# Hybrid encoder layer: value blocks multiplied in pairs of 512 columns, small tiles kept in the second weight slot

## The chip, the cores and the metric

One core of a Trainium2 chip runs the kernel in one launch. The metric is the device time of one execution in microseconds (us), the median of several executions. The core has a matrix engine (TensorE, PE), which reads on-chip memory (SBUF) and writes accumulation banks (PSUM); a vector engine (VectorE, DVE); a scalar engine (ScalarE, ACT); a general engine (GpSimd, POOL); and a sync engine (SyncE, SP) that issues most transfers.

## The reference

One layer of an encoder, sequence 2048, width 1024, all in float32:

```
mod = silu(c) @ w_ada + b_ada;  shift, scale, gate = split(mod, 3)
h   = rmsnorm(x, norm_w) * (1 + scale) + shift
proj = h @ w_in + b_in          # 4 attention parts, 5 mLSTM parts, 16 gate columns
attention: 8 heads of 64, on a 32 x 64 grid, 8 x 16 neighbourhood, bias table rpb, softmax
           times silu(z)
mLSTM:     4 heads of 128, q and k through a 5-tap convolution and silu, both directions,
           stabilised by log-gates; (fwd + bwd) * sigmoid(o), normalised per head, times silu(z)
out = rmsnorm(x + gate * (concat(attention, mLSTM) @ w_out), final_norm_w)
```

The mLSTM values and the output gates `o` of one head form one 256-column block of the projection (blocks 0 to 3), the attention's values two more (blocks 4 and 5), the mLSTM's k and q four (blocks 6 to 9, with the convolution).

## The kernel before, in words

**Numbers.** A float32 product is made of three matmuls. Each operand is split in a high part in the fast format fp32r and a low part, the rest; high x high, high x low and low x high are summed in PSUM (`mm3`, lines 638 to 640). With a depth of 1024 in eight slices that is 24 matmuls for one output tile. h lies in SBUF for the whole first phase, in four groups g of 512 tokens (`hhi`, `hlo`).

**Weights.** A block of weights is 1024 x 256. `raw_w` loads it in two halves of 512 KB into two raw buffers (line 203) and returns for each half a function that writes the high part (ACT, line 207) and the low part (DVE, line 208) into a weight slot. There are two slots, a and b; block n uses slot n % 2. Slot a has 272 columns, for the gate columns of block 0, and lives until the end; slot b is given up after the convolution.

**Start.** `start` stands in `manual_schedule`: there each engine's order is the order of the program text. It multiplies blocks 0 and 1 for all four token groups and block 2 for group 0. In its last group `next_w` loads and splits block 2 into slot a. Table fills (`table_fills`, line 758) and the store of each group's results (line 721, deferred to a later point by `defer` and `flush`) go out on SP as well.

**Value blocks.** `tok_blocks` does the rest of blocks 2 to 5, one block after the other, each by groups and each group by four tiles of 128 tokens: 24 matmuls with 256 moving columns, the tokens of h being the stationary operand, then one DVE addition of the bias out of PSUM (`vo_group` for blocks 2 and 3, line 710; `nav_group` for 4 and 5, line 673). The PSUM pool `pp` has four banks. The splits for the next block follow groups 1 and 2 of the present one. After each tile one step of `self.chain` is taken: first the gate computations (`gate_chain`, with exponential and logarithm at lines 827 and 828 and their user at line 830) mixed with the row of the output gate (`gate_row`: the vector c is loaded at line 587 and goes through Silu at line 588; lines 596 to 607), then the decay matrices (`decays`). Two stage tiles hold results until they are stored. Outside `manual_schedule` the framework's scheduler sets each engine's order, by priority and by its own estimates of when things are ready.

**Convolution and mixer.** `conv_blocks` multiplies blocks 6 to 9 with 512 moving columns. In `phase1b` the mLSTM runs per head in two passes (`ml_pass1`: states; `ml_pass2`: outputs, chunk by chunk), while `pump` lays matmuls of the remaining projections (line 1094, 512 moving columns) between its steps. Pass 1 loads a tile `kv` per chunk and multiplies its values by a weight, in place for one direction. Pass 2 fills a tile `hm` of four chunks (two buffers; lines 1366 to 1368), normalises it, transposes it on PE, and `end` (line 1407) multiplies the transposed group into the gate tile `zt` (two buffers), which is stored (line 1410) and then loaded anew (line 1326).

**Attention.** `phase2` stands in `manual_schedule` from `slot(0)` on. Per unit it makes scores on PE, adds a bias table and takes minima on DVE (line 1598), exponentials on ACT, sums, transposes on PE and values. The probabilities and their transposes go round a ring of ten tiles of 512 columns, four of them the buffers of `hm` and `zt`:

```python
for t in ring[4:] + ring[:4]:
    nc.gpsimd.memset(t, 0.0)
```

The bias tables of the first patch are loaded before `self.close()`, which ends the mixer.

Of the kernel before, what the change touches and what calls it, by code (L numbers as in the profile page):

```python
# [15 lines left out]
P = 128  # L16
# [3 lines left out]
NG = 4  # L20
# [38 lines left out]
class Kernel:  # L59
# [75 lines left out]
    def phase1(self):  # L135
        nc, tc = self.nc, self.tc
        left = ExitStack()
        right = ExitStack()
        ht012 = self.pool(left, "ht012", bufs=1)
        self.hpools = {g: ht012 for g in range(3)}  # L140
        self.hhi, self.hlo = [], []
        self.token_tiles(0)

        self.gcols = self.pool(right, "gcols", bufs=1, side="right")
        wa = self.pool(right, "wa", bufs=1, side="right")
        self.raw = self.pool(right, "raw", bufs=1, side="right")
# [3 lines left out]
        wb = self.pool(r1a, "wb", bufs=1, side="right")  # L150
        self.wslot = []
# [20 lines left out]
        self.tok_blocks(self.pool(toks, "chain", bufs=1, side="right"))  # L172
# [16 lines left out]
    def stage_tile(self, name):  # L189
        self.stages.reverse()  # L190
        return self.stages[1].tile([P, 1032], F32, tag="st", name=name).rearrange("p (o c) -> p o c", o=4)

    def load_w(self, blk, slot, halves=(0, 1)):
        for part in self.raw_w(blk, slot, halves):
            part()

    def raw_w(self, blk, slot, halves=(0, 1)):
        nc = self.nc
        hi, lo = self.wslot[slot]

        def part(half):
# [12 lines left out]
        return [part(half) for half in halves]  # L214

    def start(self, left):
# [316 lines left out]
        self.chain = iter(())  # L533
# [132 lines left out]
    def nav_group(self, blk, slot, g):  # L666
        nc = self.nc
        c0 = (blk - 4) * 256
        st = self.stage_tile(f"stv_{blk}_{g}")
        for o in range(4):  # L670
# [3 lines left out]
            next(self.chain, None)  # L674
            if o == 1:
                self.flush()
        dst = self.d_vna[g * GT : (g + 1) * GT, c0 : c0 + 256].rearrange("(o p) c -> p o c", p=P)
        self.defer(lambda: nc.sync.dma_start(dst, st[:, :, :256]))
# [17 lines left out]
    def vo_group(self, h, slot, g, first=None, brow=None, tops=(), stage=None):  # L696
# [5 lines left out]
        for o in range(4):  # L702
# [10 lines left out]
            next(self.chain, None)  # L713
            if o == 1:
                self.flush()
        nc.scalar.activation(st[:, :, 129:257], st[:, :, 129:257], AF.Sigmoid)
        dst = self.d_ck[h, 4 * g : 4 * g + 4, :, 128:385].rearrange("o p c -> p o c")
        if g == 0 and h < 3:
            (nc.scalar if h == 0 else nc.sync).dma_start(dst, st[:, :, 0:257])
        else:  # L720
            self.defer(lambda: nc.sync.dma_start(dst, st[:, :, 0:257]))

# [52 lines left out]
    def tok_blocks(self, chain_pool):  # L775
        self.wide = chain_pool.tile([P, 2 * D], F32, name="wide")
        self.chain = itertools.chain(self.gate_both(chain_pool), self.decays(chain_pool))
        order = [2, 3, 4, 5]
        next(self.chain)
        r = self.tables_begin(chain_pool)  # L780
        for n, blk in enumerate(order):
            parts = self.raw_w(blk + 1, (blk + 1) % 2)
            if blk < 5:
                self.load_bias(blk + 1)
            for g in range(1 if blk == 2 else 0, NG):
                if blk < 4:
                    self.vo_group(blk, blk % 2, g)
                else:
                    self.nav_group(blk, blk % 2, g)
                if g in (1, 2):  # L790
                    parts[g - 1](self.nc.vector)
                if blk == 2 and g == 3:
                    self.tables_bias(r)
# [4 lines left out]
    def gate_chain(self, pool, gates):  # L798
# [29 lines left out]
        nc.scalar.activation(a, a, AF.Ln, bias=1.0)  # L828
        lf = new("lf")
# [369 lines left out]

    def close(self):  # L1200
# [45 lines left out]
    def ml_pass1(self, ml, h):  # L1246
# [5 lines left out]
        def load(k):  # L1252
            t = tiles[k] = ml.tile([P, 257], F32, tag="kv", bufs=7, name=f"kv_{h}_{order[k]}")
            nc.sync.dma_start(t, self.d_ck[h, order[k], :, 0:257])

        def weight(k):
            c = order[k]
            v = tiles[k][:, 128:257]
            sides[k] = {d: v for d in range(2) if 0 <= c + 1 - 2 * d < NC}
            if len(sides[k]) == 2:  # L1260
                sides[k][1] = ml.tile([P, 129], F32, tag="wv", bufs=4, name=f"wv_{h}_{c}")
# [45 lines left out]
    def ml_pass2(self, ml, h):  # L1307
# [11 lines left out]
        def load_z(gi):  # L1319
# [4 lines left out]
            else:  # L1324
                t = self.mle.tile([P, 4, CH], F32, tag="zt", bufs=2, name=f"zt_{h}_{gi}")
# [135 lines left out]
    def phase2(self):  # L1461
# [91 lines left out]
        tabs = [p.tile([P, 960], F32, name=f"tab{i}") for i in range(4)]  # L1553
# [182 lines left out]
        for i in range(2):  # L1736
            load_q(i)
            for u in (2 * i, 2 * i + 1):
                load_tab(b0, u, nc.sync if i else nc.gpsimd)
        self.close()  # L1740
        pss = ExitStack()
# [3 lines left out]
        ring = [few.tile([P, 512], F32, tag=tag, bufs=bufs, name=f"ring_{i}") for i, (tag, bufs) in enumerate((("hm", 2), ("hm", 2), ("zt", 2), ("zt", 2)))]  # L1745
        ring += [p.tile([P, 512], F32, name=f"ring_{i}") for i in range(4, 10)]
        for t in ring[4:] + ring[:4]:
            nc.gpsimd.memset(t, 0.0)
# [118 lines left out]
        with self.tc.manual_schedule():  # L1867
            for m in range(len(patches) + 1):
# [96 lines left out]
```

## Time and profile before

| | |
|---|---|
| time, median of 3 runs | 1277.23 us (1277.06 to 1277.59) |
| the profiled execution's own time | 1276.39 us |
| its span, first to last instruction | 1274.5 us |
| PE busy | 1264.4 us, 99% |
| DVE / ACT / POOL busy | 790.3 / 537.7 / 201.7 us |
| granted TensorE clock, mean | 0.999 of full speed |

The stages on PE: start up to about 131 us, value blocks to 306, convolution to 491, mixer with projections to about 927, attention with the output projection to the end. An engine's busy time is the sum of its instructions' records; PE's records overlap one another, so the distance between starts says more than a record's length.

### The profile page before, as it was taken

To read this page: it belongs to the slowest core of one execution; us is meant where nothing else is said; L and a number is where in the kernel's file an instruction comes from. 1 tells how busy PE (TensorE), PEld (TensorE's weight loads), DVE (VectorE), ACT (ScalarE), POOL (GpSimd) and SP (SyncE) were. 2 spreads that over 40 slices of the span, in tenths; PEclk is the share of its full clock that TensorE was granted. 3 is DMA by queue.
4 is the path that set the end of the run, shared out by engine and by line. 5 is a ranking of instruction groups with operands and counts; after the bars stand their busy time and mean duration, and the time that the engine had idled before them with its cause. 6 is when DMAs were issued, how large, how long until landed. Compare 5 with 4: busy or idle time off the path is not lost.

```text
span 1274.5 us, 22948 instructions
## 1 busy us (share of the span) xinstructions
PE 1264.4 (99%) x8168; PEld 1095.4 (86%) x8168; DVE 790.3 (62%) x2391; ACT 537.7 (42%) x1182; POOL 201.7 (16%) x368
## 2 busy tenths in 40 slices
PE   9999999999999999999999999999999999999997
PEld 8999999999888888888888888888877888888886
DVE  7875542213667664267777778777556766767664
ACT  6642425442334222123323323324357565565552
POOL 0000003440000000000001001000424331332541
PEclk9999999999999999999999999999999999999999
DMA  9999947996678764745757867746677755655551
GB/s 366 335 309 286 283 147 198 249 245 180 180 180 189 165 154 115 207 131 164 204 160 207 251 189 215 240 149 186 207 249 266 230 162 160 203 177 176 176 173 67
DMA packets 217082, 259.08 MB, mean 203 GB/s; under 512 B 23435, under 2 KB 163595, under 8 KB 216968
## 3 DMA queue, kind: packets, MB, share of 16 engines
q1 hardware_dynamic: 149542, 190.09, 52.1%
q0 software_dynamic: 13616, 37.28, 8.9%
q10 hardware_dynamic: 53810, 30.24, 8.4%
q8 instruction: 65, 1.06, 0.3%
q14 instruction: 49, 0.40, 0.1%
HBM read 173.05 MB, written 92.72 MB: 209 GB/s over the span
## 4 chain that ended last, share of the span: by engine, by line
PE 95%; DVE 2%; ACT 1%; issue 1%; DMA 0%; DVEq 0%; ACTq 0%
PE pq L1094 27%; PE y L1676 14%; PE pc L639 5%; PE pc L640 5%; PE pc L638 5%; PE pO L1633 4%; PE pT L1618 3%; PE pvo L638 3%; PE pvo L640 3%; PE pvo L639 3%; PE pS L1587 3%; PE pvo L693 3%; PE pv L640 2%; PE pv L639 2%; PE pv L638 2%; PE pi L1346 2%
## 5 line engine op out<-in xcount | busy, mean ns | idle before, releaser
L1094 PE MATMUL pq<-hhi,whi_a 128*128 128x512 f32 x512 | 208.4, 407 | 0.0
L1094 PE MATMUL pq<-hlo,whi_a 128*128 128x512 f32 x512 | 207.8, 406 | 0.0
L1094 PE MATMUL pq<-hhi,wlo_a 128*128 128x512 f32 x512 | 207.2, 405 | 0.0
L1368 POOL TENSOR_TENSOR hm<-hm,ck 128x128 f32<-128x128 f32 x64 | 28.2, 440 | 580.3 <-DVE hm L1367 541.0
L1094 PEld LDWEIGHTS pq<-hhi,wlo_a 128*128 128x128 f32 x512 | 96.8, 189 | 16.7 <-issue 0.2
L1094 PEld LDWEIGHTS pq<-hlo,whi_a 128*128 128x128 f32 x512 | 96.7, 189 | 16.1 <-issue 0.4
L1094 PEld LDWEIGHTS pq<-hhi,whi_a 128*128 128x128 f32 x512 | 96.8, 189 | 15.9
L1599 ACT ACTIVATE ring<-ring,mn 128x480 f32<-128x480 f32 (+5 forms) x128 | 75.9, 594 | 55.8 <-DVE mn L1598 55.8
L1620 ACT ACTIVATE ring<-pT 96x384 f32<-96x384 f32 (+3 forms) x128 | 65.8, 514 | 63.5 <-PE pT L1618 62.0
L1676 PE MATMUL y<-hhi,wlo_a 128*128 128x512 f32 (+1 forms) x272 | 87.0, 394 | 0.2 <-ACT y L1683 0.2
L1676 PE MATMUL y<-hhi,whi_a 128*128 128x512 f32 x256 | 86.2, 408 | 0.0
L1349 ACT ACTIVATE num<-px,gtile 128x129 f32<-128x129 f32 x120 | 38.7, 367 | 105.2 <-PE px L1344 91.5
L1522 POOL DMA_DIRECT2D v<-d_vna x158 | 78.7, 505 | 15.6 <-issue 4.4
L1618 PEld LDWEIGHTS pT<-ident,ring 128*128 128x128 f32 (+2 forms) x416 | 51.1, 136 | 19.2 <-ACT ring L1620 3.7
L1618 PE MATMUL pT<-ident,ring 128*128 128x128 f32 (+2 forms) x416 | 66.2, 272 | 0.0
L638 PE MATMUL pvo<-whi_b,hhi 128*128 128x256 f32 x224 | 63.6, 284 | 0.0
L1598 DVE CUSTOM_DVE_ANT_0 ring<-pS,tab 128x480 f32<-128x480 f32 (+5 forms) x128 | 61.9, 539 | 2.6 <-PE pS L1587 2.4
L640 PE MATMUL pvo<-whi_b,hlo 128*128 128x256 f32 x224 | 63.1, 282 | 0.0
L639 PE MATMUL pvo<-wlo_b,hhi 128*128 128x256 f32 x224 | 63.0, 281 | 0.0
L934 ACT ACTIVATE dec<-dec,gtile 128x128 f32<-128x128 f32 x128 | 41.3, 391 | 46.9 <-POOL dec L927 43.2
L673 DVE TENSOR_TENSOR stv<-pv,brow 128x256 f32<-128x256 f32 x32 | 13.6, 425 | 71.8 <-PE pv L640 71.8
L710 DVE TENSOR_TENSOR stvo<-pvo,brow 128x256 f32<-128x256 f32 x60 | 24.7, 418 | 50.7 <-PE pvo L640 40.0
(343 smaller groups left out, 3331.3 us busy)
## 6 DMA issues: line engine op xcount, KB each, us to landing
ck<-d_ck SPq DMA_DIRECT2D x64, 384.5 KB, 3.6
rawq<-in_w_main_dram SPq DMA_DIRECT2D x28, 512.0 KB, 5.2
raw<-in_w_main_dram SPq DMA_DIRECT2D x18, 512.0 KB, 6.2
kv<-d_ck SPq DMA_DIRECT2D x64, 128.5 KB, 3.0
dec<-d_mneg SPq DMA_DIRECT2D x32, 256.0 KB, 6.0
d_ck<-dec ACTq DMA_DIRECT2D x32, 256.0 KB, 6.9
qs<-d_qna SPq DMA_DIRECT2D x30, 256.0 KB, 3.9
xr<-in_x_p_dram POOLq DMA_DIRECT2D x15, 512.0 KB, 3.9
```

Of the source, the lines that this page charges most:

```text
L638: nc.tensor.matmul(ps, lhi(k), rhi(k), start=(k == 0), stop=False)
L639: nc.tensor.matmul(ps, lhi(k), rlo(k), start=False, stop=False)
L640: self.mark = nc.tensor.matmul(ps, llo(k), rhi(k), start=False, stop=(k == KT - 1))
L934: nc.scalar.activation(t[:, o, :], t[:, o, :], AF.Exp, bias=self.cols["g"][:, d, h, c : c + 1])
L1094: self.mark = nc.tensor.matmul(patch_ps(ps) if patch else ps, w, self.htok(h, g, k, patch), start=(k == 0 and n == 0), stop=(k == KT - 1 a ...
L1522: queue.dma_start(chunks[key][r * nkc : (r + 1) * nkc, :], rows[r])
L1598: nc.vector.tensor_tensor_reduce(pt[:, :nk], ps, tabs[ct][:, j * nk : (j + 1) * nk], 1.0, 3e38, ALU.add, ALU.min, mn)
L1599: nc.scalar.activation(pt[:, :nk], pt[:, :nk], AF.Exp, bias=mn, scale=-1.0, accum_out=sums[:, j : j + 1])
L1618: nc.tensor.transpose(ps[:cs, i, :], U[u][j][:, i * cs : (i + 1) * cs], self.ident)
L1620: nc.scalar.activation(t[:cs, :nch, :], ps[:cs, :nch, :], AF.Copy)
L1633: nc.tensor.matmul(po[j * HD : (j + 1) * HD, ct, :], v[:n, h * HD : (h + 1) * HD], pt[j][:n, i, :], start=(i == 0), stop=(i == nch - 1))
L1676: nc.tensor.matmul(y, m[:, k, :], w[k][:, cs], start=(k == 4 and n == 0), stop=(k == 3 and n == 2))
```

## The change

Blocks 2 and 3, and blocks 4 and 5, are multiplied together where both are at hand: one matmul has 512 moving columns, 256 from each slot, and fills a whole PSUM bank (`pair_group`). The order of groups becomes (2,1) (3,0) [2+3: 2] [2+3: 3] (3,1) (4,0) [4+5: 1] [4+5: 2] [4+5: 3] (5,0). Each block's raw halves are loaded and split at other points (`splits`, `turns`; the raw halves of block 3 in `next_w`). Four stage tiles take the place of two in that stage. The two weight slots become the halves of one tile per part, which stays to the end. Once the convolution is done, slot 2 holds the `kv` tiles, the `zt` tiles and the four bias tables (`spare`); the values weighted in pass 1 all go to tiles of their own; `end` writes into `hm` and that is stored; the fourth table is loaded after `close()`. In `gate_chain` a step ends between the logarithm and its user. The ring keeps the two `hm` buffers and eight tiles of its own, and DVE clears the upper half of each, in the written order.

```diff
@@ phase1
-        for nm, pl in (("a", wa), ("b", wb)):
-            self.wslot.append(tuple(pl.tile([P, KT, 272 if nm == "a" else 256], F32R, name=f"w{part}_{nm}") for part in ("hi", "lo")))
+        self.wpair = tuple(wa.tile([P, 2, KT, 272], F32R, name=f"w{part}") for part in ("hi", "lo"))
+        self.wslot = [tuple(part[:, j] for part in self.wpair) for j in range(2)]
...
+        held, more = self.stages, self.pool(toks, "stage2", bufs=2, side="right")
+        self.stages = [*held, more, more]
@@ start, next_w
-            for part in self.raw_w(2, 0):
+            self.parts = []
+            for half, part in enumerate(self.raw_w(2, 0)):
                 yield
                 part(nc.vector)
+                self.parts.append(self.raw_part(3, 1, half))
@@ new
+    def pair_group(self, blk, g):
+        sts = [self.stage_tile(f"st2_{blk + j}_{g}") for j in range(2)]
+        hi, lo = self.wpair
...
+        for o in range(4):
+            ps = self.pp.tile([P, GT], F32, tag="pp", name=f"p2_{blk}_{g}_{o}")
+            self.mm3(
+                ps.rearrange("p (a c) -> p a c", a=2),
+                lambda k: self.hhi[g][:, k, o * P : (o + 1) * P],
+                lambda k: self.hlo[g][:, k, o * P : (o + 1) * P],
+                lambda k: hi[:, :, k, :256],
+                lambda k: lo[:, :, k, :256],
+            )
+            for j, st in enumerate(sts):
+                row, part = self.brows[(blk + j) % 2], ps[:, 256 * j : 256 * j + 256]
...
+                    self.evicted = nc.vector.tensor_add(st[:, o, :256], part, row)
+                next(self.chain, None)
+            next(self.mid, None)
+            if o == 1:
+                self.flush()
@@ tok_blocks
-        order = [2, 3, 4, 5]
+        order = [(2, 1), (3, 0), (2, 2), (2, 3), (3, 1), (4, 0), (4, 1), (4, 2), (4, 3), (5, 0)]
+        both = ((2, 2), (2, 3), (4, 1), (4, 2), (4, 3))
+        def splits(rest, after):
+            for _ in range(rest):
+                yield
+            for part in self.parts:
+                part(self.nc.vector)
+                yield
+            if after:
+                self.parts = self.raw_w(*after)
...
+        turns = {0: (1, (4, 0)), 4: (0, (5, 1)), 5: (0, (6, 0)), 9: (0, None)}
@@ gate_chain
         nc.scalar.activation(a, a, AF.Ln, bias=1.0)
+        yield
         lf = new("lf")
@@ new
+    def spare(self, half, start, n):
+        return self.wslot[1][half].rearrange("p a b -> p (a b)").bitcast(F32)[:, start : start + n]
@@ ml_pass1
-            t = tiles[k] = ml.tile([P, 257], F32, tag="kv", bufs=7, name=f"kv_{h}_{order[k]}")
+            t = tiles[k] = self.spare(0, k % 7 * 257, 257)
...
+            sides[k] = {d: ml.tile([P, 129], F32, tag="wv", bufs=8, name=f"wv_{h}_{c}_{d}") for d in range(2) if 0 <= c + 1 - 2 * d < NC}
@@ ml_pass2
-                t = self.mle.tile([P, 4, CH], F32, tag="zt", bufs=2, name=f"zt_{h}_{gi}")
+                t = self.spare(1, gi % 2 * 512, 512).rearrange("p (a q) -> p a q", q=P)
...
-            nc.vector.scalar_tensor_tensor(z, ps, self.mlw[:, h : h + 1], z, ALU.mult, ALU.mult)
-            src = zt[gi]
+            src = hm[gi]
+            nc.vector.scalar_tensor_tensor(src.rearrange("p a q -> p (a q)"), ps, self.mlw[:, h : h + 1], z, ALU.mult, ALU.mult)
@@ phase2
-        tabs = [p.tile([P, 960], F32, name=f"tab{i}") for i in range(4)]
+        tabs = [self.spare(half, start, 960) for half, start in ((0, 0), (0, 960), (1, 1024), (1, 0))]
...
         self.close()
+        load_tab(b0, 3)
...
-        for t in ring[4:] + ring[:4]:
-            nc.gpsimd.memset(t, 0.0)
+        ring += [p.tile([P, 512], F32, name=f"ring_{i}") for i in range(2, 10)]
...
         with self.tc.manual_schedule():
+            for t in ring:
+                nc.vector.memset(t[:, 256:], 0.0)
```

## Rows read from the trace of the kernel before

**Rows 1.** The page: PE's busy line, and the chain that ended last, by engine.

```profile
PE 1264.4 (99%) x8168; PEld 1095.4 (86%) x8168; DVE 790.3 (62%) x2391; ACT 537.7 (42%) x1182; POOL 201.7 (16%) x368
...
PE 95%; DVE 2%; ACT 1%; issue 1%; DMA 0%; DVEq 0%; ACTq 0%
```

**Rows 2.** The waits of PE, first of five rows: us in total, times, longest.

```profile
PE pvo L436 <- ACT hhi L404: 1.2, 2, 0.8
```

**Rows 3.** Tile pv (blocks 4, 5): ns min/median/max, first and last start.

```profile
L638 PE MATMUL pv<-whi_a,hhi x128: 276/280/283, 215.0 to 260.0; 128*128 128x256 f32 x128
...
L638 PE MATMUL pv<-whi_b,hhi x128: 279/281/285, 260.4 to 305.6; 128*128 128x256 f32 x128
```

**Rows 4.** The chain in order of time, convolution and projections: start, us, what.

```profile
306.09 0.23 PE pc L638
...
309.59 0.23 PE pc L638
...
491.53 41.70 PE pq L1094 x180
```

**Rows 5.** Tile pvo, PE, 119 to 215 us: block 2 in slot a.

```profile
L638 PE MATMUL pvo<-whi_a,hhi x96: 277/280/388, 130.6 to 166.3; 128*128 128x256 f32 x96
```

**Rows 6.** DVE in order of time, 115 to 200 us; in brackets the idle time before.

```profile
129.16 1.23 DVE L208 TENSOR_TENSOR wlo_a<-raw,whi_a 128x1024 fp32r<-128x1024 f32 x1 [3.60 <-ACT whi_a L207]
...
130.63 1.21 DVE L208 TENSOR_TENSOR wlo_a<-raw,whi_a 128x1024 fp32r<-128x1024 f32 x1
...
138.18 0.29 DVE L830 SCALAR_TENSOR_TENSOR wide<-wide 128x128 f32<-128x128 f32 x1 [1.08 <-ACT wide L828]
...
152.56 1.22 DVE L208 TENSOR_TENSOR wlo_b<-raw,whi_b 128x1024 fp32r<-128x1024 f32 x1 [5.31 <-ACT whi_b L207]
153.71 0.42 DVE L710 TENSOR_TENSOR stvo<-pvo,brow 128x256 f32<-128x256 f32 x1
```

**Rows 7.** SP's transfer issues in order of time, 95 to 310 us.

```profile
120.43 0.91 SPq L203 DMA_DIRECT2D raw<-in_w_main_dram  x2
121.45 1.15 SPq L721 DMA_DIRECT2D d_ck<-stvo  x1
122.65 9.32 SPq L758 DMA_DIRECT2D d_t<-big  x2
133.05 4.41 SPq L721 DMA_DIRECT2D d_ck<-stvo  x1
137.55 0.88 SPq L587 DMA_DIRECT2D cact<-in_small_dram  x1
...
145.73 1.11 SPq L203 DMA_DIRECT2D raw<-in_w_main_dram  x2
```

**Rows 8.** ACT in order of time, 110 to 310 us.

```profile
128.06 1.06 ACT L207 ACTIVATE whi_a<-raw 128x1024 fp32r<-128x1024 f32 x1 [7.24 <-DMA raw<-in_w_main_dram]
...
143.26 0.21 ACT L588 ACTIVATE cact<-cact 128x8 f32<-128x8 f32 x1 [3.81 <-DMA cact<-in_small_dram]
```

**Rows 9.** Mixer, head 0: DVE and SP in order of time, 590 to 616 us.

```profile
596.08 0.29 DVE L1366 TENSOR_SCALAR hm<-num,r 128x128 f32<-128x128 f32 x1
...
597.54 0.37 SPq L1326 DMA_DIRECT2D zt<-d_zml  x1
```

**Rows 10.** A group of memsets (mean ns); POOL and DVE in time.

```profile
L114 DVE MEMSET ones<- 128x128 f32 x1 | 0.2, 165 | 0.8 <-PEq L1952 0.8
...
908.02 3.37 POOL L1748 MEMSET ring<- 128x512 f32 x7
...
920.69 0.75 DVE L1137 SCALAR_TENSOR_TENSOR qst<-pq,bcol,qst 128x512 fp32r<-128x512 f32 x1
922.10 0.55 POOL L1755 DMA_DIRECT2D m<-d_mix  x1 [6.55 <-DMA d_mix<-zt_last]
925.02 0.75 DVE L1137 SCALAR_TENSOR_TENSOR qst<-pq,bcol,qst 128x512 fp32r<-128x512 f32 x1 [3.59 <-ACT qst L1136]
927.96 0.46 DVE L1598 CUSTOM_DVE_ANT_0 ring<-pS,tab 128x288 f32<-128x288 f32 x1 [2.18 <-PE pS L1587]
```

More of the change, by code (lines that the diff above doesn't have):

```diff
@@ L170, in phase1 @@
         self.sp = self.pool(ps1a, "sp", bufs=1, space=PSUM)
-        self.tok_blocks(self.pool(toks, "chain", bufs=1, side="right"))
+        chain_pool = self.pool(toks, "chain", bufs=1, side="right")
+        held, more = self.stages, self.pool(toks, "stage2", bufs=2, side="right")
+        self.stages = [*held, more, more]
+        self.tok_blocks(chain_pool)
+        self.stages = held
         toks.close()
@@ L189, in stage_tile, with raw_w, raw_part @@
     def stage_tile(self, name):
[L190 to L197, printed above, removed]
+        self.stages.append(self.stages.pop(0))
+        return self.stages[-1].tile([P, 1032], F32, tag="st", name=name).rearrange("p (o c) -> p o c", o=4)
+    def raw_w(self, blk, slot):
+        return [self.raw_part(blk, slot, half) for half in range(2)]
+    def raw_part(self, blk, slot, half):
         nc = self.nc
         hi, lo = self.wslot[slot]
-        def part(half):
+        if True:
             raw = self.raw.tile([P, 4, 256], F32, tag=f"raw{half}", name=f"raw_{blk}_{half}")
@@ L212, in part @@
             return run
-        return [part(half) for half in halves]
     def start(self, left):
@@ L674, in nav_group, with stored @@
             next(self.chain, None)
+            next(self.mid, None)
             if o == 1:
                 self.flush()
-        dst = self.d_vna[g * GT : (g + 1) * GT, c0 : c0 + 256].rearrange("(o p) c -> p o c", p=P)
-        self.defer(lambda: nc.sync.dma_start(dst, st[:, :, :256]))
+        self.stored(blk, g, st)
+    def pair_group(self, blk, g):
+        nc = self.nc
+        sts = [self.stage_tile(f"st2_{blk + j}_{g}") for j in range(2)]
+        hi, lo = self.wpair
+        if blk < 4:
+            for st in sts:
+                nc.gpsimd.memset(st[:, :, 128:129], 1.0)
+        for o in range(4):
[9 more added lines that the diff above has]
+                row, part = self.brows[(blk + j) % 2], ps[:, 256 * j : 256 * j + 256]
+                if blk < 4:
+                    pair = st[:, o].rearrange("p (j c) -> p j c", j=2)[:, :, 0:128]
+                    self.evicted = nc.vector.tensor_add(pair, part.rearrange("p (j c) -> p j c", j=2), row.rearrange("p (j c) -> p j c", j=2))
+                else:
+                    self.evicted = nc.vector.tensor_add(st[:, o, :256], part, row)
+                next(self.chain, None)
+            next(self.mid, None)
+            if o == 1:
+                self.flush()
+        for j, st in enumerate(sts):
+            self.stored(blk + j, g, st)
+    def stored(self, blk, g, st):
+        nc = self.nc
+        if blk < 4:
+            nc.scalar.activation(st[:, :, 129:257], st[:, :, 129:257], AF.Sigmoid)
+            dst, src = self.d_ck[blk, 4 * g : 4 * g + 4, :, 128:385].rearrange("o p c -> p o c"), st[:, :, 0:257]
+        else:
+            c0 = (blk - 4) * 256
+            dst, src = self.d_vna[g * GT : (g + 1) * GT, c0 : c0 + 256].rearrange("(o p) c -> p o c", p=P), st[:, :, :256]
+        if g == 0 and blk < 3:
+            (nc.scalar if blk == 0 else nc.sync).dma_start(dst, src)
+        else:
+            self.defer(lambda: nc.sync.dma_start(dst, src))
     def load_bias(self, blk):
@@ L713, in vo_group @@
             next(self.chain, None)
+            next(self.mid, None)
             if o == 1:
                 self.flush()
[L716 to L721, printed above, removed]
+        self.stored(h, g, st)
     def tables_begin(self, pool):
@@ L777, in tok_blocks @@
         self.chain = itertools.chain(self.gate_both(chain_pool), self.decays(chain_pool))
-        order = [2, 3, 4, 5]
         next(self.chain)
         r = self.tables_begin(chain_pool)
[L781 to L793, printed above, removed]
+        order = [(2, 1), (3, 0), (2, 2), (2, 3), (3, 1), (4, 0), (4, 1), (4, 2), (4, 3), (5, 0)]
+        both = ((2, 2), (2, 3), (4, 1), (4, 2), (4, 3))
+        self.load_bias(3)
+        def splits(rest, after):
[6 more added lines that the diff above has]
+                self.parts = self.raw_w(*after)
+                if after[0] == 5:
+                    self.load_bias(4)
+                if after[0] == 6:
+                    self.load_bias(5)
+        turns = {0: (1, (4, 0)), 4: (0, (5, 1)), 5: (0, (6, 0)), 9: (0, None)}
+        for n, (blk, g) in enumerate(order):
+            group = self.vo_group if blk < 4 else self.nav_group
+            self.mid = splits(*turns[n]) if n in turns else iter(())
+            if (blk, g) in both:
+                self.pair_group(blk, g)
+            else:
+                group(blk, blk % 2, g)
+            for _ in self.mid:
+                pass
+            if n == 2:
+                self.tables_bias(r)
         for _ in self.chain:
@@ L1744, in phase2 @@
         pO = self.pool(pss, "pO", bufs=1, space=PSUM)
[L1745 to L1748 removed]
+        ring = [few.tile([P, 512], F32, tag=tag, bufs=bufs, name=f"ring_{i}") for i, (tag, bufs) in enumerate((("hm", 2), ("hm", 2)))]
+        ring += [p.tile([P, 512], F32, name=f"ring_{i}") for i in range(2, 10)]
         order = itertools.cycle(ring)
```

10 lines of the change are left out of this document (2 added, 8 removed).

## The prediction

> **What bounds the kernel now.** I read the page first. TensorE (PE) is busy 99% of the span and supplies 95% of the chain that ended last [rows 1]. Next I read what PE itself waits for: the view lists five waits, and the largest is 1.2 us in all [rows 2]. So nothing is to be won by removing a wait. Time can only come from fewer or denser matmul starts, or go into a wait that PE does not have today. Busy durations are no help, because a matmul's record overlaps the next one's (a 256-column one is 281 ns long); what counts is the distance from start to start. Last I read the engines around two places where the change moves a dependency close to PE: 119 to 166 us (block 3's weights) and 905 to 930 us (the passage to attention).
>
> The sum is made against the profiled execution: span 1274.5, and 1.89 us around it, 1276.39. The runs' median is 0.84 us higher, 1277.23; I apply the difference to the median. About 0.2%, 2.55 us, is what a measurement of this kernel can tell from no change.
>
> **Part 1, pairs of 512 columns.** Today a value block is multiplied in tiles of 24 matmuls with 256 moving columns. Block 4's 384 matmuls start at 215.0 and block 5's at 260.4: 45.4 / 384 = 118.2 ns each [rows 3]. Block 5 ends where the convolution's first matmul starts, 306.09 [rows 4]: 45.7 / 384 = 119.0. Together 91.1 / 768 = 118.6 ns. Two of them, which one 512-column matmul replaces, cost 237.2 ns.
>
> The trace has no matmul of this form (tokens as weights, two runs of 256 columns moving), so I bound it by the two nearest 512-column streams. The undisturbed run of the output-side projections takes 41.70 / 180 = 231.7 ns; the start of the convolution 15 steps in 3.50 us (306.09 to 309.59), 233.3 ns [rows 4]. The diff pairs two groups of blocks 2/3 and three of 4/5: 5 groups x 4 tiles x 24 = 480 matmuls in place of 960. The gain is 480 x (237.2 - 231.7) = 2.6 us at one end and 480 x (237.2 - 233.3) = 1.9 at the other; with the spread of the 256-column rate (118.2 to 119.0) the outer bounds are 1.5 and 3.0. I take 2.6, the long run's, since 180 steps weigh more than 15. It lies wholly on the critical engine.
>
> [...]
>
> Evictions stay two VectorE (DVE) adds of 256 columns per token tile, 0.42 us each [rows 6]. A pair tile holds one PSUM bank for 24 x 0.232 = 5.6 us of matmuls instead of 2.85, so with four banks DVE gets about twice the slack. The two extra stage tiles remove waits of the small ones-columns on GpSimd (POOL), which hide under PE: 0.
>
> **Part 2, block 3's weights sooner.** Block 2's first group starts at 130.6 [rows 5] and lasts 96 x 0.1186 = 11.4 us. Today two more groups of block 2 follow, so block 3 is needed at 165; its first half is split from 152.56 [rows 6]. After, group (3,0) comes second, at 142.0. Its raw halves can be fetched only when block 2's splits release the buffers: the first split ends at 129.16 + 1.23 = 130.4, the second at 131.8 [rows 6]. The start section has a written order, so the sync queue (SP) now stands at these two loads, and the store and the two table fills that went out at 121.45 to 131.97 [rows 7] go behind them. That is in their favour: the previous raw load, issued at 120.43 into a full queue, let ScalarE (ACT) start at 128.06, 7.6 us later [rows 7, 8]; for that issued at 145.73, DVE's split started at 152.56, right behind ACT's copy of 1.06, so ACT started at 151.5, 5.8 us later [rows 6, 7].
>
> First half: issued 130.4, landed 136.2 to 138.0, copied by ACT (1.06), split by DVE (1.23): 138.5 to 140.3 against 142.0, so 1.7 to 3.5 us of cover. Second half: SP has the 1.15 us store in between, so issued about 132.1, landed 137.9 to 139.7, split by 140.2 to 142.0; it is needed from the 13th matmul, 142.0 + 1.4 = 143.4: cover 1.4 to 3.2 us. I cost it at 0. With cover gone each us late is a us on PE.
>
> The yield after the logarithm fits this. The exponential and the logarithm now share ACT with the two copies, and DVE already waits 1.08 us for the logarithm today [rows 6]. One tile later, that wait stands behind one more eviction instead of in front of it: 0 on PE, and the split behind it keeps its cover.
>
> Moved with this, the fills (9.32 us of issue) and a store (4.41) now precede the conditioning vector's load, which goes out at 137.55 today [rows 7]: I estimate 8 us later. ACT's Silu of it waited until 143.26 [rows 8] and would wait until about 151. Behind it stand sigmoids and gate work, not PE, provided the copies stand ahead of it.
>
> **Part 3, blocks 4, 5, 6.** Their raw loads get one to three groups of lead, 8 us or more, against landings of 5.8 to 7.6: 0, with the same price if late.
>
> **Part 4, small tiles in slot 2.** The state tiles' and gate tiles' loads, the weighted values and their matmuls keep their number: 0. The last table now loads after the mixer's end instead of before it; its place is free before the last group's store, seen done at 922.10, and its data are used after 927.96 [rows 10]: 0. One new wait: the normalised group is written into its own tile and stored from there, so the tile two groups later waits for that store. Head 0: the first group's store is seen done at 597.54, when its gate tile is loaded anew, and the third group's first DVE write is at 596.08 [rows 9]. So DVE would stand 1.5 us, at two places per head, 8 in all: up to 12 us of DVE time, which PE covers with projection matmuls. At 0.
>
> **Part 5, the ring.** Ten POOL clears of 512 columns leave; ten DVE clears of 256 come. DVE clears 128 columns in 0.165 us, POOL 512 in 3.37 / 7 = 0.48 [rows 10]: for 256 the bounds are 0.17 and 0.33, twice the 128; I take 0.27, 2.7 us in all. They stand in DVE's written order ahead of the first score reduction at 927.96. The second ring tile is the last group's tile, whose store is seen done at 922.10 [rows 10]. DVE is free from there to 925.02 and again from 925.77 to 927.96: 5 us for them. At 0.
>
> Sum: -2.6, all else hidden: 1277.2 - 2.6 = **1274.6 us**.
>
> **Rivals.**
> *Block 3's copies behind the Silu (slower).* If the scheduler puts ACT's copies behind the Silu, they start near 151.2 and the second split ends near 151.2 + 1.06 + 1.06 + 1.23 = 154.6; the first near 153.5, 11.5 us after PE needs it. Net 11.5 - 2.6 = +9: 1286. It turns slower than before when the split is 2.6 us late, by over 0.2% at 5.2 us. For it: today ACT stands 3.81 us at exactly this Silu. Against: the copies wait for nothing but loads issued earlier. 6%.
> *The second half only a little late.* Same place; a landing of 7.6 us and a store that takes 4.41 instead of 1.15 us to issue put the split at 145.2: 1.8 us of stall, 1276.4; a landing one us worse, 1277.4. With smaller and somewhat larger stalls, 1275.6 to 1280: 15%.
> *The passage.* DVE waits at the second ring tile until 922.10, and an eviction of 0.75 us, now at 920.69 [rows 10], stands behind it, behind the eight clears (2.2) and behind a split of 1.2: it ends by 926.3. The next group's eviction comes at 925.02, ACT's half of it some 0.7 before, so PE has ended that group by 924.3 and, with two banks, wants the first one back. 2 us back: 1276.6. If the clears only push the score reductions, 0.8 us. 12%. [...]
> *The pairs do not get denser.* If two runs of columns cost nearly what two 256-column matmuls cost now, the gain is 0 to the lower outer bound of part 1, 1.5: 1275.7 to 1277.2. 5%. [...]
> *The tile wait reaches PE.* 8 x 1.5 = 12 us, net +9.4: 1286.6. Against: one projection group (5.6 us) of cover. 4%.
> *More than forecast.* Freed waits let the scheduler place mixer work better, 1 to 2 us: 1273. 8%.
>
> **How the numbers follow.** The forecast's own case, 1273.7 to 1275.6, has 50%; the bound of 0.2% (1274.7) runs through it, and I put three fifths of it on the faster side, since the uninterrupted 512-column run alone reaches the bound. Faster: 30 + 8 = 38%. Slower by over 0.2%: 6 + 4 + 3 (the top of the small stalls) = 13%. Same: 20 + 12 + 12 + 5 = 49%. For 8 in 10 I leave out the two 1286 cases (10%), the top of the small stalls and the lowest tail: 1272.3 to 1279.0.
>
> **What would show it.** Right: a pair tile's 24 matmuls take 5.56 to 5.60 us; no wait of PE in the value stage or the mixer; the value stage ends 2 to 3 us sooner. Wrong: PE waiting for block 3's split at 142 to 147; PE waiting for an eviction near 924.5; DVE at the store's landing with PE idle in the mixer; or pair matmuls 237 ns apart.

## The result, and the profile after

The changed kernel takes **1282.78 us** (median of 6 runs, 1281.39 to 1285.42); the kernel before, run beside it, 1277.14. The ratio is 1.0045, 95% interval 1.0031 to 1.0059: slower, by 5.6 us, where 1274.6 was forecast and 1279.0 was the upper end of the range. The profiled execution is one of the long ones, 1284.72 us against 1276.39, so the stages below add up to 8.3 us and not to the 5.6 of the medians.

The top of its page, and what PE waited for:

```profile
span 1282.9 us, 22072 instructions
## 1 busy us (share of the span) xinstructions
PE 1264.9 (99%) x7688; PEld 1072.1 (84%) x7688; DVE 785.9 (61%) x2401; ACT 538.5 (42%) x1183; POOL 195.1 (15%) x358
```

```profile
engine line waited for: us in total, times, longest us
PE pvo L639 <- DVE ends L901: 3.1, 1, 3.1
PE kt L1099 <- ACT acc_k L1090: 3.1, 3, 2.1
...
PE ht L1455 <- ACT hm L1448: 0.6, 2, 0.5
PE pi L1401 <- DVE num L1406: 0.4, 1, 0.4
```

Against [rows 2] the first two lines are new; PE has 480 instructions fewer and is no less busy. Where the time went is seen by stage. The table gives, for each execution with a profile, where the value stage's first gate transpose starts on PE, and the lengths up to the first matmul of the convolution (`pc`), of the projections (`pq`), of the scores (`pS`) and to the last matmul; the other rows are the experiments below.

| us | starts | value | convolution | mixer | attention |
|---|---|---|---|---|---|
| before | 133.5 | 172.5 | 185.4 | 435.8 | 340.4 |
| after | 133.7 | 174.7 | 189.2 | 437.7 | 340.3 |
| x1 splits sooner | 137.4 | 170.3 | 187.1 | 437.0 | 340.4 |
| x2 no step end | 133.4 | 173.5 | 185.0 | 437.4 | 340.5 |
| x3 block 6 copied by DVE | 136.1 | 172.1 | 189.3 | 438.3 | 340.3 |
| x4 x1 and x3 | 133.7 | 171.9 | 187.3 | 437.1 | 340.3 |
| y1 old value stage | 133.9 | 172.2 | 185.0 | 437.7 | 340.3 |
| y2 x1 and x2 | 136.0 | 170.0 | 185.0 | 437.3 | 340.3 |
| y3 y2, bias row sooner | 137.8 | 170.0 | 185.0 | 437.2 | 340.4 |
| y4 y3 unpaired | 134.5 | 172.3 | 185.0 | 436.9 | 340.3 |
| z1 y3, three tiles | 133.5 | 170.0 | 185.0 | 436.1 | 340.4 |
| z2 before, start filled | 135.5 | 172.5 | 185.4 | 436.3 | 340.3 |
| z3 z1, start filled | 133.8 | 170.0 | 185.0 | 436.0 | 340.4 |
| z4 y1, three tiles | 135.6 | 172.2 | 185.1 | 435.9 | 340.3 |

After less before, row by row: 0.2, 2.2, 3.8, 1.9 and -0.1, with some 0.5 behind the last matmul: 8.5 by these rounded figures, for 8.3 us between the two executions. Three stages lose.

**Value stage.** VectorE's timeline around PE's wait, then ScalarE's:

```profile
start us, us, engine line op out<-in xcount [idle before <-releaser]
...
138.28 1.22 DVE L208 TENSOR_TENSOR wlo<-raw,whi 128x1024 fp32r<-128x1024 f32 x1
142.98 0.29 DVE L884 SCALAR_TENSOR_TENSOR wide<-wide 128x128 f32<-128x128 f32 x1 [3.48 <-ACT wide L881]
...
145.21 0.42 DVE L892 TENSOR_TENSOR_SCAN wide<-ones,wide 64x128 f32<-64x128 f32 x1
145.66 0.43 DVE L753 TENSOR_TENSOR stvo<-pvo,brow 128x256 f32<-128x256 f32 x1
146.01 1.22 DVE L208 TENSOR_TENSOR wlo<-raw,whi 128x1024 fp32r<-128x1024 f32 x1
```

```profile
138.66 1.05 ACT L207 ACTIVATE whi<-raw 128x1024 fp32r<-128x1024 f32 x1
139.72 1.28 ACT L880 ACT_TABLE_LOAD   x1
...
142.64 0.31 ACT L881 ACTIVATE wide<-wide 128x128 f32<-128x128 f32 x1
```

Block 3's second half is copied by 139.71, in time for PE. Its split starts only at 146.01, because the user of the gate logarithm (L884) stands ahead of it in VectorE's order and waits 3.48 us for ScalarE, and seven more steps of the gate chain and an eviction follow. PE and its clock, by PE's timeline and by windows (of the columns: busy time of PE, PEld, DVE, ACT, POOL, then the granted clock):

```profile
143.87 0.28 PE L638 MATMUL pvo<-whi,hhi 128*128 128x256 f32 x1
147.28 0.58 PE L639 MATMUL pvo<-wlo,hhi 128*128 128x256 f32 x1 [3.13 <-DVE ends L901]
```

```profile
130.00:143.80 13.80, 13.80 (x120) 13.80 (x119) 5.40 (x14) 8.92 (x11) 0.10 (x1) 1.00 0.97 254
144.00:147.30 3.30, 0.17 (x3) 0.02 (x1) 3.12 (x9) 0.00 (x0) 0.00 (x0) 0.94 1.13 316
147.30:150.50 3.20, 3.20 (x15) 3.20 (x16) 0.97 (x3) 2.49 (x3) 0.00 (x0) 0.52 1.07 360
150.50:155.00 4.50, 4.50 (x40) 4.50 (x39) 1.99 (x4) 0.71 (x1) 0.10 (x1) 1.00 0.86 156
```

The wait is 3.13 us, 3.3 by the starts (147.28 less 143.87 is 3.41, less the usual 0.12). The row names L901 because that ended last; what the matmul reads is the split, which ended at 147.23. Behind the wait stand 15 matmuls at 0.52 of the clock, 0.21 us apart instead of 0.12, another 1.4 us.

How long PE waits here differs between executions. Experiment x3 has the same code in this stage; its start took 2.4 us longer, PE came later to block 3, waited 1.92 us (until 148.45) and kept its full clock behind that:

```profile
PE pvo L642 <- DVE ends L904: 1.9, 1, 1.9
```

```profile
148.40:152.00 3.60, 3.55 (x30) 3.55 (x31) 1.50 (x5) 2.82 (x3) 0.10 (x1) 1.00 1.06 346
```

Its stage ends at 308.3, that of the changed kernel at 308.5: what the start took longer, the wait took less.

**Convolution.** ScalarE's timeline where block 6 is copied, and what the sync queue waited for between 297 and 320:

```profile
305.40 0.99 ACT L988 ACTIVATE dec<-dec,gtile 128x128 f32<-128x128 f32 x3
306.42 0.37 ACTq L990 DMA_DIRECT2D d_ck<-dec  x1
306.83 2.01 ACT L207 ACTIVATE whi<-raw 128x1024 fp32r<-128x1024 f32 x2 [0.44 <-ACT dec L988]
315.54 1.06 ACT L207 ACTIVATE whi<-raw 128x1024 fp32r<-128x1024 f32 x1 [6.70 <-DMA raw<-in_w_main_dram]
318.10 1.06 ACT L207 ACTIVATE whi<-raw 128x1024 fp32r<-128x1024 f32 x1 [1.50 <-DMA raw<-in_w_main_dram]
319.06 0.67 ACT L1051 ACTIVATE u<-pc,bcol 128x512 f32<-128x512 f32 x1
```

```profile
SPq L203 <- DMA d_ck<-dec: 5.3, 1, 5.3
SPq L203 <- DVE stv L672: 4.3, 2, 2.9
```

Block 6 used to be copied at 266.6 and 268.7, inside the stage. Now its slot is taken until the last pair tile ends at 297, and its copies stand behind the last decay matrix, at 306.83. Block 7's raw buffers come free later for that, and by the profile the queue also stands at their loads (L203) until a store of the decay matrices is through (why a load of weights stands for that store is not shown). ScalarE's first step of the convolution (L1051) stands behind the copies of block 7 in ScalarE's order. VectorE's first convolution step starts at 320.4 instead of 312.5; it works off that lag while PE waits three times for a k group to turn. From the stage's first matmul it is 11.9 us to this step, and 9.5, 10.1 and 11.0 in x1, x3 and x4, the other three that lose here; in the ten profiles without the loss it is 6.6.

**Mixer.** VectorE waits for the store of the tile `hm` two groups before:

```profile
DVE hm L1421 <- DMA d_mix<-hm: 8.8, 8, 1.7
```

### The profile page after: what moved, and what is told of

Its sections match the earlier page's. It is cut to its first block, busy times and chain, and to the rows that moved or that the text cites. A ratio compares the mean times of both kernels' runs of the same rounds, so it can differ in the third digit from the quotient of the medians.

```text
span 1282.9 us, 22072 instructions
## 1 busy us (share of the span) xinstructions
PE 1264.9 (99%) x7688; PEld 1072.1 (84%) x7688; DVE 785.9 (61%) x2401; ACT 538.5 (42%) x1183; POOL 195.1 (15%) x358
## 4 chain that ended last, share of the span: by engine, by line
PE 69%; DMA 10%; DVE 4%; ACT 3%; issue 2%; SPq 1%; POOL 0%; ACTq 0%; DVEq 0%; POOLq 0%
PE pq L1148 25%; PE y L1731 14%; DMA d_ck<-dec 4%; PE pO L1688 4%; PE pT L1673 3%; PE pc L639 3%; PE pc L638 3%; PE pc L640 3%; PE pS L1642 3%; DMA wraw<-in_w_out_dram 2%; PE pi L1401 2%; PE dc L1338 2%; PE px L1399 2%; DMA dec<-d_mneg 1%; ACT dec L988 1%
## 5 line engine op out<-in xcount | busy, mean ns | idle before, releaser
L1148 PE MATMUL pq<-hlo,whi 128*128 128x512 f32 x512 | 208.4, 407 | 0.0
L1148 PE MATMUL pq<-hhi,whi 128*128 128x512 f32 x512 | 208.1, 407 | 0.0
L1148 PE MATMUL pq<-hhi,wlo 128*128 128x512 f32 x512 | 207.2, 405 | 0.0
L1148 PEld LDWEIGHTS pq<-hhi,whi 128*128 128x128 f32 x512 | 96.8, 189 | 16.3
L1148 PEld LDWEIGHTS pq<-hhi,wlo 128*128 128x128 f32 x512 | 96.8, 189 | 16.3 <-issue 0.2
L1148 PEld LDWEIGHTS pq<-hlo,whi 128*128 128x128 f32 x512 | 96.8, 189 | 16.1 <-issue 0.4
L638 PE MATMUL pc<-hhi,whi 128*128 128x512 f32 x256 | 102.0, 398 | 0.0
L639 PE MATMUL pc<-hlo,whi 128*128 128x512 f32 x256 | 101.3, 396 | 0.0
L640 PE MATMUL pc<-hhi,wlo 128*128 128x512 f32 x256 | 100.6, 393 | 0.1
L1731 PE MATMUL y<-hhi,wlo 128*128 128x512 f32 (+1 forms) x272 | 87.0, 394 | 0.2 <-ACT y L1738 0.2
```

The lines of the kernel that those rows point to most:

```text
L638: nc.tensor.matmul(ps, lhi(k), rhi(k), start=(k == 0), stop=False)
L639: nc.tensor.matmul(ps, lhi(k), rlo(k), start=False, stop=False)
L640: self.mark = nc.tensor.matmul(ps, llo(k), rhi(k), start=False, stop=(k == KT - 1))
L1148: self.mark = nc.tensor.matmul(patch_ps(ps) if patch else ps, w, self.htok(h, g, k, patch), start=(k == 0 and n == 0), stop=(k == KT - 1 a ...
L1731: nc.tensor.matmul(y, m[:, k, :], w[k][:, cs], start=(k == 4 and n == 0), stop=(k == 3 and n == 2))
```

## The experiments

All ran beside the kernel before (1277.1, 1277.2 and 1277.2 in the three sets). A median mixes executions whose start took 2 to 4 us longer with others (last section), so the stages above say more than the medians.

**x1: block 3's splits one tile sooner.**
```diff
-        turns = {0: (1, (4, 0)), ...
+        turns = {0: (0, (4, 0)), ...
```


> The changed kernel with block 3's two splits one token tile sooner each, so that in VectorE's order the second split stands ahead of the user of the gate logarithm instead of behind it. In the changed kernel's trace VectorE stood 3.48 us at that user, then did 3.03 us of scans, and PE stood 3.13 us at 143.87 and ran its next 13 matmuls 0.21 us apart instead of 0.12. Theory A (two separate losses: VectorE's order at block 3, and ScalarE's order at block 6): PE's wait at 144 goes, 3.3 + 1.3 = 4.6 us, the waits for k transposes in the convolution (3.6 us) stay: 1282.8 - 4.6 = 1278.2 (1277 to 1280). Theory B (one loss: the late block 3 pushes all that follows and so makes the convolution's waits too): both go, 1282.8 - 8.2 = 1274.6. Theory C (the second raw half lands too late for any order): no gain, PE's wait stays at 144, 1282.8.

1280.12 us, ratio 1.0019 (1.0009 to 1.0028). PE's wait at 144 is gone, the value stage is 170.3: theory A for this stage, C is out. The waits for k transposes shrink from 3.1 us to one of 1.7, and the convolution from 189.2 to 187.1: block 3 pushes part of that loss, as B said, but not all of it. The median lies 0.1 us above A's range.

**x2: no step end after the logarithm.**
```diff
         nc.scalar.activation(a, a, AF.Ln, bias=1.0)
-        yield
```


> The changed kernel without the step end between the gate logarithm and its user. The user then stands ahead of both splits of block 3 in VectorE's order. Theory A (the wait for the logarithm holds whatever stands behind it in VectorE's order, and the step end only chose which half that is): the first split comes after about 143.3 and the second still behind the scans, so PE waits about as long, now at the first matmuls of the group: 1282 to 1284. Rival (the step end itself made the loss): PE's wait at 144 goes or halves, 1278 to 1280.

1279.97, ratio 1.0021 (1.0012 to 1.0030). PE's waits from 130 to 500:

```profile
PE pvo L639 <- DVE ends L900: 2.1, 1, 2.1
PE pvo L639 <- DVE wlo L208: 0.9, 1, 0.9
```

The wait for block 3 stays, cut in two, as theory A said. That the convolution's waits vanish no theory had: the time is 2 us under theory A's and inside the rival's range, but not by the rival's way, since the wait at block 3 did not halve. The gate columns' matmuls (`ps_cols`) now start at 163.4 instead of 170.5, the decay matrices end at 297.2 instead of 306.4, and block 6 is copied right behind them:

```profile
297.24 0.37 ACTq L989 DMA_DIRECT2D d_ck<-dec  x1
297.65 2.01 ACT L207 ACTIVATE whi<-raw 128x1024 fp32r<-128x1024 f32 x2 [0.44 <-ACT dec L987]
```

**x3: block 6 copied by VectorE.**
```diff
-                nc.scalar.activation(hi[:, ks, :256], raw, AF.Copy)
+                if blk == 6:
+                    nc.vector.tensor_copy(hi[:, ks, :256], raw)
+                else:
+                    nc.scalar.activation(hi[:, ks, :256], raw, AF.Copy)
```


> The changed kernel with the copies into the high part of block 6 done by VectorE instead of ScalarE, nothing else. In the changed kernel's trace ScalarE did them at 306.83, behind the last decay matrix, although block 6's slot was free from 297; block 7's loads, its splits and the first convolution step on VectorE (320.4, before 312.5) followed from it. Theory A (ScalarE's order at block 6 causes the convolution's waits): VectorE's first convolution step comes 5 us or more sooner, PE's waits for k transposes (3.6 us in all) shrink to under 1 us, PE's wait at 144 stays: 1282.8 - 3.1 = 1279.7 (1279 to 1280.5). Rival D (the output weights land late because more transfers are under way, and VectorE stands at them): block 6 is split sooner, but the waits for k transposes stay: 1282.8.

1282.4, ratio 1.0038 (1.0025 to 1.0050): theory A falls here, and time and waits are those of rival D: block 6 is split 8 us sooner, and PE waits 3.6 us for k transposes. D's reason does not hold: VectorE's waits for the output weights between 297 and 400 are 26.1 us here and 25.6 in the changed kernel, but also 23.3 before and 26.2 in y3, where the convolution loses nothing. VectorE's timeline, the queue, and ScalarE's first step of the convolution:

```profile
300.27 1.21 DVE L211 TENSOR_TENSOR wlo<-raw,whi 128x1024 fp32r<-128x1024 f32 x1
303.11 2.01 DVE L211 TENSOR_TENSOR wlo<-raw,whi 128x1024 fp32r<-128x1024 f32 x1
313.55 1.22 DVE L211 TENSOR_TENSOR wlo<-raw,whi 128x1024 fp32r<-128x1024 f32 x1 [4.67 <-ACT whi L210]
```

```profile
SPq L1005 <- DMA d_ck<-dec: 7.6, 2, 6.1
SPq L203 <- DMA d_ck<-dec: 4.5, 1, 4.5
SPq L724 <- DMA d_ck<-dec: 3.9, 1, 3.9
```

```profile
317.01 0.69 ACT L1054 ACTIVATE u<-pc,bcol 128x512 f32<-128x512 f32 x1 [2.15 <-DMA d_ck<-dec]
```

The way over ScalarE's order was closed, and the same lateness came by the other: the queue stood behind stores of decay matrices 4.5 us at block 7's load, and 7.6 us at the load of the output gate's row, and ScalarE's first convolution step itself waited for the last of these stores, issued at 307.80.

**x4: both.**


> Both edits of the two runs before: block 3's splits one token tile sooner, and block 6's copies on VectorE. Theory A: both losses go, 4.6 + 3.1 to 3.6: 1282.8 - 7.9 = 1274.9 (1274 to 1276), faster than the kernel before (1277.1) by 0.1 to 0.25%. Theory B: the same as the first run alone, 1274.6. Rival D or C: 1278 or more.

1279.36, ratio 1.0021 (1.0009 to 1.0033): above A's and B's times. 1278 or more was said for C and D; x1 rules out C, and D's reason fell in x3. The value stage is 171.9 and not 170: VectorE's first addition of block 3 waits for its bias row.

```profile
155.83 0.42 DVE L756 TENSOR_TENSOR stvo<-pvo,brow 128x256 f32<-128x256 f32 x1 [2.77 <-DMA brow<-in_b_row_dram]
```

A new theory for the convolution fits the first four: it loses where the decay matrices end 0.5 to 3.2 us ahead of it (after 2.1, x1 3.2, x3 0.5, x4 1.3 us), not where they end 9.7 ahead (x2; before 12.7). In the runs below they end 6.2 to 12.5 us ahead, and none loses.

**y1: the value stage of before with the rest of the change.** `order = [2, 3, 4, 5]`, the old loop over blocks and groups, the old `next_w`, no step end.


> The changed kernel with the value stage of the kernel before (blocks one after the other, tiles of 256 columns, the old points for loads and splits, no step end after the gate logarithm), and all else of the change: small tiles in slot 2, the weighted values in tiles of their own, the group written into hm, the ring cleared by VectorE. In five profiles of the changed kernel and of the first four runs the mixer took 437.0 to 438.3 us from the first projection matmul to the first score, in that of the kernel before 435.8, attention 340.3 in all. Theory M (these small-tile edits cost the mixer 1.2 to 1.9 us of their own): 1277.1 + 1.5 = 1278.6, mixer 437 or more. Theory N (the mixer pays for the disturbed stages ahead of it, the edits cost nothing): 1277.1, mixer 435.8.

1278.1, ratio 1.0009 (1.0000 to 1.0017), mixer 437.7: theory M. The small-tile edits cost the mixer 1.9 us in this profile.

**y2: x1 and x2 together.**


> The changed kernel with block 3's splits one token tile sooner and without the step end after the gate logarithm. The first removed PE's wait at 144 (value stage 170.3 and 171.9 us in two profiles, before 172.5, changed 174.7). The second let the decay matrices end at 297 instead of 306, and the convolution took 185.0 us in that profile (before 185.4, changed 189.2). Theory A2 (the late decay matrices make the convolution's waits; the two losses add up): 1282.8 - 2.8 to 4.4 - 4.1 = 1274.3 to 1275.9. Rival (what is left in the value stage is taken by the wait for block 3's bias row, 2.4 us of PE in one profile, and the mixer keeps its 1.5): 1277 to 1278. Rival (the convolution's waits come and go from run to run, whenever the decay matrices end): 1278.5 or more.

1278.09, ratio 1.0003 (0.9994 to 1.0012). By stages theory A2: value 170.0, convolution 185.0, the two losses add up, and PE waits in neither stage. The median is 2 us over A2's and next to the first rival's, of which one half holds: the mixer keeps its loss. The profile's start took 2.5 us longer.

**y3: y2 with block 3's bias row sooner.**
```diff
+        self.load_bias(3)
         next(self.chain)
         r = self.tables_begin(chain_pool)
...
-        self.load_bias(3)
```


> The run before with block 3's bias row loaded ahead of the gate weights and the last table fills instead of behind them. In the run with both edits VectorE's first addition for block 3 stood 2.77 us until 155.83 at this row, issued at 150.5, and PE then waited 1.7 + 0.7 us for banks. If that wait is real and is the last one in the value stage, 1.5 to 2.5 us less than the run before and a value stage of 170 us: 1273.5 to 1276. If PE's banks cover it once the convolution's waits are gone, no difference.

1277.37, ratio 0.9994 (0.9985 to 1.0004), value stage 170.0 as in y2: no difference there. Of the 2.4 us that the expectation names, 0.7 lie at 107, ahead of the stage; whether the other 1.7 would come back with a quicker start was not separated.

**y4: y3 with the pairs taken apart.**
```diff
-            self.mm3(
-                ps.rearrange("p (a c) -> p a c", a=2),
...
+            for j in range(2):
+                self.tok_tile(ps[:, 256 * j : 256 * j + 256], self.wslot[(blk + j) % 2], 4 * g + o)
```


> The run before this one, with every pair tile multiplied as two tiles of 256 columns into the two halves of the same bank; order, loads, splits and evictions stay. Theory (a 512-column matmul starts 231.7 to 234.6 ns after the last, two of 256 columns 237.2): 480 x 2.6 to 5.5 ns = 1.2 to 2.6 us slower than the run before, and more only if a tile of 48 matmuls holds a bank too long. Rival (the pairs are worth nothing, the gain comes from the order): the same time.

1278.28, ratio 1.0009 (1.0001 to 1.0018). The value stage is 172.3 against 170.0: 2.3 / 480 = 4.8 ns a pair. By the tiles' starts: a tile of blocks 4 and 5 comes every 5.68 us here (250.01, 255.69, 261.37) and every 5.56 in the changed kernel (252.64, 258.20, 263.76). The pairs are the whole gain of the stage; the new order alone (172.3) is worth nothing against the old (172.5).

**z1: y3 with three tiles `hm`.**
```diff
-hm[gi] = self.mle.tile([P, 4, CH], F32, tag="hm", bufs=2, ...
+hm[gi] = self.mle.tile([P, 4, CH], F32, tag="hm", bufs=3, ...
```
The ring takes the third in place of one of its own.


> The run with the bias row loaded sooner, and three tiles hm in place of two (the ring takes the third in place of one of its own). In the four runs before, VectorE stood at hm until the store of the group two before was through (8.0 us in 8 waits in the run with the old value stage), and PE waited 0.9 to 1.4 us for hm's transposes (0.2 in the kernel before). Theory P (part 4's new wait reaches PE): VectorE's waits for that store go, PE's waits for hm fall to about 0.2, the mixer from 437.2 to 436.2 us or less, the time by about 1 us. Rival (the transposes wait for other work of VectorE and ScalarE): the mixer stays at 437.

**1274.48** (1273.00 to 1276.76), ratio 0.9973 (0.9963 to 0.9984): theory P, and faster than both kernels. VectorE no longer waits at `hm`, and PE's waits have no line above 0.4 us behind the start:

```profile
PE y L1730 <- DVE hlo L1623: 0.4, 1, 0.4
PE ht L1454 <- ACT hm L1447: 0.4, 1, 0.4
PE pq L1147 <- DVE qst L1190: 0.3, 1, 0.3
```

The median fell 2.9 us from y3's, the mixer 1.1. Most of the rest is luck with the start, 133.5 here and 137.8 in y3's profile: among runs with a mean granted clock of 0.998 or more (which leaves out the executions with a long drop: the seven profiles with a drop in the start have 0.994 to 0.997), y3's three have a median of 1274.83 and z1's five one of 1274.08, and such runs are 3 of 11 there and 5 of 7 here. Against the kernel before the gain is no such luck: its 16 runs with that clock have a median of 1277.0.

**z4: y1 with three tiles `hm`.**


> The run with the old value stage, and three tiles hm. That run took 1278.1 us and its mixer 437.7. Theory P: mixer 436 to 436.6, 1277.0. Rival: mixer stays above 437, 1278.

1276.88, ratio 0.9994 (0.9985 to 1.0003), mixer 435.9 instead of 437.7: theory P again, with the rest of the kernel as it was.

**z2 and z3: a filled start**, on the kernel before and on z1.
```diff
-        for n in range(10):
-            if n == 7:
-                for j, ps in enumerate(wide):
+        for n in range(11):
+            for j, ps in enumerate(wide):
+                if n == 7 + 2 * j:
```


> The kernel before, with its start alone changed: the warming matmuls of the first 7 us (results unused) stand between the two broadcasts of c as well, and there is one more. In profiles of four of the eight experiments the granted clock fell to half at 9.5 to 11.5 us and stayed there for 8 to 13 us, which put the first projection matmul at 17.0 to 18.9 us instead of 14.1 to 14.8; the code of the start is the same in all of them, and about one in six runs of the kernel before lies 1.5 us or more over its median. Theory S (that spread is this drop): the runs close up at the low end, median 1276.6 to 1277.0, nothing above 1278. Rival (other transfers make the spread): spread and median as before, 1277.2.

> All mends on the changed kernel: block 3's splits sooner, no step end after the logarithm, bias row sooner, three tiles hm, and the filled start of the run before this one. From the stages of the profiles: value stage 170.0 (before 172.5), convolution 185.0 (185.4), mixer 436.2 (435.8), attention 340.3 (340.4): 1276.4 - 2.6 = 1273.8 for an execution with no drop of the clock in the start; with theory S right, median 1273.5 to 1274.5, faster than the kernel before by 0.2 to 0.3%. If the drop stays: 1275 to 1277.

1278.61, ratio 1.0006 (0.9997 to 1.0014), and 1275.9, ratio 0.9989 (0.9980 to 0.9998). The edit did not remove the drop (0.81 of the clock from 10 to 19 us in z2's profile) and more runs of it lie high, 7 of 11 above 1278 (of the kernel before beside it 8 of 29). As a mend it failed, and it does not decide theory S. The clocks on record speak for S: of the 90 runs of the kernel before in the three sets, the 21 with a mean granted clock of 0.996 took 1278.4 to 1280.1 us, the 69 with 0.997 or more 1275.8 to 1278.6. Where in a run the clock fell is known only for the profiled ones.

## Why the prediction was wrong

**Part 1 was right.** Forecast 2.6 us, bounds 1.5 to 3.0. Without the waits the value stage is 2.5 us shorter (172.5 to 170.0 in y2, y3 and z1), and y4 puts 2.3 of it on the pairs. The first sign came as said: a pair tile every 5.56 us. One reading was off: 306.09 in [rows 4] is not the convolution's first matmul, which starts at 305.93; with it a 256-column matmul takes 118.4 to 118.5 ns, and the same sum gives 2.5.

**Part 2 failed at one sentence:** that the wait for the logarithm "stands behind one more eviction instead of in front of it: 0 on PE, and the split behind it keeps its cover". The landings were sized well: the copies ran at 135.74 and 138.66, against 136.2 to 138.0 and 137.9 to 139.7. But the split behind the logarithm's user was block 3's own second half. The wait had grown from 1.08 us [rows 6] to 3.48, since ScalarE did both copies, a sigmoid, the exponential and three table loads (1.28 us each) first; from its end to the split VectorE took 3.03 more, for L884, the seven gate steps behind it and an eviction. I costed the wait on its own engine and did not write out VectorE's order around it. That is 4.7 us of the value stage in this profile (174.7 to 170.0): 3.3 of waiting and 1.4 at 0.52 of the clock, which the prediction's "each us late is a us on PE" left out; in x3's profile the same code lost 2.1. The prediction's own sign of being wrong, "PE waiting for block 3's split at 142 to 147", came to the place. Here the split, whose copy was ready at 139.71, started at 146.01, behind L884 and its wait of 3.48 us. The rival "the second half only a little late" had the place but blamed the landing.

**Also part 2: "behind it stand sigmoids and gate work, not PE".** Behind the gate work stand the decay matrices, and behind these, ScalarE, the transfers and the convolution's weights. The first load of a decay matrix comes 63.9 us after the stage's start (before 54.9); without the step end 58.9, with block 3 mended 59.4 (x1), with both mends 55.3. So the late block 3 and the step end each push it by some 4 to 5 us. I costed the step end at 0 because PE waits for none of it at that point.

**Part 3 failed for block 6.** Its load had the lead that I gave it; its slot did not. Pairing keeps slot a until 297, where block 5 alone had left it free from 260, so its copies lost 30 us of lead. With the late decay matrices it cost the convolution 3.8 us; with early ones nothing (185.0 in x2, y2, y3, y4, z1 and z3, all in the new order of groups). That the decay matrices decide is shown by x2, which moved them by way of the gate chain and left block 6's code and slot as they were; how the delay is split between ScalarE's order, the queue and the transfers is not (x3 closed one way only).

**Part 4: the mechanism was right, the size was not 0.** I had the wait at eight places, 1.5 us each; VectorE waited eight times, 8.8 us in all. "PE covers with projection matmuls" failed by 1.1 us (y3 to z1) to 1.8 (y1 to z4).

**Part 5 was right.** The clears took 272 ns each (0.27 forecast), and the attention stage took 340.3 (before 340.4). VectorE stood 5.1 us at them for the last group's store, as the rival "the passage" had it, but PE did not wait there:

```profile
L1923 DVE MEMSET ring<- 128x256 f32 x9 | 2.4, 272 | 5.1 <-DMA d_mix<-hm 5.1
```

So -2.5 + 4.7 + 3.8 + 1.9 is 7.9 of the 8.3 us of the profiled execution; the runs at 1281.4 to 1281.8 have no profile, so which of the losses was smaller in them is open. Three costs at 0 were each wrong by some 2 to 5 us, each by a wait that passed from engine to engine before it reached PE. The range was too narrow for that: it held one of them at a time.

## What to carry to other kernels

An edit that is hidden today is costed by writing out the order of the engine it stands on, with everything behind it in that order, up to the first consumer on the critical engine; the load's landing is only the first term (block 3's second half was copied by 139.71 here, and its split ran at 146.01). When two tiles are joined, ask what else waited for the earlier release of either one's buffer. And where a tile is written in place of another, one more buffer is the cheap test: it took the 1.1 us back in the mixer. All four edits of z1 together (splits sooner, no step end, bias row sooner, third buffer) turned this change from 5.6 us slower into 2.7 us faster (1277.2 to 1274.48).

## What the runs showed of the hardware

The granted clock fell after a wait of PE in the changed kernel's profile, and that cost 1.4 us on top: behind 3.13 us without matmuls it was 0.52 of full for 3.2 us. Behind 1.92 us in x3 it stayed at 1.00 (148.40 to 152.00); x2, with a wait of 2.1 us, has a mean of 0.999 over its whole profile.

In the start, the clock fell to 0.50 in some executions, with PE shown busy through the whole stretch. Windows of y3's profile and, for the same stretch, of the kernel before:

```profile
10.00:19.00 9.00, 9.00 (x37) 8.37 (x35) 4.84 (x15) 4.64 (x11) 0.00 (x0) 0.50 1.01 374
```

```profile
10.00:19.00 9.00, 8.88 (x70) 8.28 (x68) 8.16 (x19) 7.07 (x13) 0.00 (x0) 1.00 0.99 373
```

37 matmuls against 70 in the same 9 us, and a start 4.3 us later. Ahead of this stretch the kernel before ran the warming matmuls, then, from 7.46 us for 1.98, the four matmul records that broadcast c from one row. What decides whether it falls stays open: the code of this stretch is the same in both, and filling the stretch did not prevent it (z2).
